# A two-layer attention trunk on one core: 22 instead of 14 opening products, and softmax sums of two heads folded together

## The chip, the cores and the metric

The kernel runs on one core of a Trainium2 chip. The metric is the time of one execution on the device in microseconds, shown for several runs. A profile of one execution gives the start and end of every instruction on TensorE (PE; its weight loads are PEld), VectorE (DVE), ScalarE (ACT), GpSimd (POOL) and SyncE (SP, which here issues all DMA transfers), and the clock that TensorE was granted.

## The reference

Input x is 2048 tokens by 1024 channels, f32. Layer A normalises x, projects it to q, k, v, one forget logit per head and a gate, normalises q and k per head, and attends causally with 16 heads of 64 channels; then output times silu(gate), output projection, residual. Layer B makes keys and values once and attends in a window of 128. The change touches layer A's attention, whose core is this:

```python
c = jnp.cumsum(log_f, axis=1)
logits = jnp.einsum('bqhd,bkhd->bhqk', qi, k) * scale
logits = logits + ci[..., :, None] - c_k[..., None, :]
logits = jnp.where(causal, logits, -jnp.inf)
p = jax.nn.softmax(logits, axis=-1)
return jnp.einsum('bhqk,bkhd->bqhd', p.astype(v.dtype), v)
```

## The kernel before, in words

One program does all: `constants`, then layer A (projections, attention, output projection), then layer B. Each f32 operand of a large product is split into a high part h that TensorE takes whole (type fp32r) and a rest lo, and a product is the sum of h·h, h·lo and lo·h: three products of 128x128 by 128x512.

**Start.** `constants` sets a tile to zero and lets TensorE multiply it by itself IDLE times (line 228), while the first transfers run. GpSimd makes masks (`select`, line 215), VectorE makes small tables from them (`fold`, `identb`, `band`, lines 239 to 254). The first projection needs weight tiles: ScalarE writes the high half (wh, line 502), VectorE the low half (wl, line 503), eight pairs for the first 128 tokens' product (line 775, psum tile b). For each block of 128 tokens ScalarE and VectorE split the transposed x (lines 395 and 396), square it (401) and sum the squares along the free axis (403, tile ro); TensorE adds up over partitions with a product by ones (line 416, psum tile pa). Pinned instructions (`keep_in_program_order`) and a scheduler that works out an order from its own costs set how these are interleaved; on the chip each engine runs its own list strictly in that order.

**Layer A's attention.** 16 heads, each with 4 chunks of 512 queries, each chunk with steps of two 128-key blocks: 20 steps a head, 320 in all (`scores`, `values`). Scores are laid out keys by queries: two products per block (lines 994 and 995, psum tile sc, three banks), exp on ScalarE (1009), high half (ScalarE, 1012), rest (GpSimd, 1013), and four products with the values three steps later (1037, psum tile pa). The row maxima that the exponent needs come from separate products and reductions a head or so ahead (949, 957, 962), and reach the operands as four small transfers (576). Diagonal blocks get the causal mask as one more product by an identity matrix: lines 999 (two blocks side by side in the last step of a chunk) and 1003. Between all that, `gate` feeds products for the gate (line 1079, psum tile pb), whose weights come in 512 KB transfers (line 1056, tile wr<-wg, two buffers).

**The sums.** A chunk's exp values are added up in an accumulator (1022), keys on partitions. At its end `sums` reduces 32x32 blocks transposed: 16 columns of partial sums per chunk, 64 per head, in the tile `part`, which holds two heads. Five steps after a head's last chunk, `recips` folds them:

```python
nc.tensor.matmul(ps, part[:, h % 2, c0:c1].rearrange("p c b -> p (c b)"), self.fold, ...)   # L922
rc = self.sb("sq", [nr, 32])
nc.vector.tensor_tensor(rc, ps, roots[:nr, 1 if c0 else 0], ALU.mult)                       # L927
nc.vector.reciprocal(rc, rc)                                                                # L928
```

The stationary operand is 64 columns of `part`, the moving one the 128x32 table `fold`; the result, 64 partitions by 32, takes a bank of sc. It is multiplied by the inverse norms of the tokens (`roots`, loaded and inverted early, lines 1112 and 1113), inverted, and stored to `rd` by SP (929). Head 15 does it in two calls, so that its last chunk alone is left at the end. The output projection reads `rd` back, for heads 0 to 3 from step 284 on.

Of the kernel before, what the change touches and what calls it, by code (L numbers as in the profile page):

```python
# [14 lines left out]
BF16 = mybir.dt.bfloat16  # L15
# [8 lines left out]
P = 128  # L24
# [4 lines left out]
H = 16  # L29
# [3 lines left out]
CH = 512  # L33
NCH = S // CH
EPS = 1e-6
NEG = -1e30
ROT = 16
# [5 lines left out]
SUM_LAG = 5  # L43
# [25 lines left out]
EARLY = 40  # L69
REST_AT = 3  # L70

IDLE = 14

VECTORS_AT = 8
ANGLES_AT = 11
# [78 lines left out]
class Trunk:  # L154
# [56 lines left out]
    def constants(self):  # L211
        nc, cp, a = self.nc, self.const, self.a

        def select(view, src, pattern, base, cm, fill):
            nc.gpsimd.affine_select(
                out=view, in_=src, pattern=pattern, compare_op=ALU.is_ge,
                fill=fill, base=base, channel_multiplier=cm,
            )

        def tile_(name, shape, dt=F32):  # L220
            return cp.tile(shape, dt, name=name, tag=name)

        idle = self.sb("sq", [P, CH], F32R)
        nc.vector.memset(f_(idle), 0.0)
        ps = self.ps("pb", [P, CH])
        for i in range(IDLE):
            self.tc.keep_in_program_order(
                nc.tensor.matmul(ps, idle[:, :P], idle, start=i == 0, stop=i == IDLE - 1)
            )

        self.ones = tile_("ones", [P, P])
        nc.gpsimd.memset(self.ones, 1.0)
        self.tri = tile_("tri", [P, P])
        select(self.tri, self.ones, [[1, P]], 0, -1, 0.0)
        self.ident = tile_("ident", [P, P])
        select(self.ident, self.tri, [[-1, P]], 0, 1, 0.0)

        self.fold = tile_("fold", [P, 32])
        nc.vector.tensor_tensor(self.fold, self.ident[:, :32], self.ident[:, 32:64], ALU.add)
        for c in (64, 96):  # L240
            nc.vector.tensor_tensor(self.fold, self.fold, self.ident[:, c : c + 32], ALU.add)
        nc.vector.tensor_single_scalar(self.fold, self.fold, 2.0, ALU.mult)
        self.identb = tile_("identb", [P, P], BF16)
        nc.vector.tensor_copy(self.identb, self.ident)

        self.mask_s = tile_("mask_s", [P, 2, P], BF16)
        nc.gpsimd.memset(self.mask_s, 0.0)
        for i in range(2):
            select(self.mask_s[:, i], self.mask_s[:, i], [[1, P]], 0, -1, NEG)

        self.band = tile_("band", [P, 2, P], BF16)
        nc.gpsimd.memset(self.band[:, 0], 0.0)
        select(self.band[:, 0, :], self.band[:, 0, :], [[-1, P]], 0, 1, NEG)
        nc.vector.tensor_tensor(self.band[:, 1], self.tri, self.ident, ALU.subtract)

        self.loads = []
        warm = tile_("warm", [P, 1])
        nc.scalar.activation(warm, self.ones[:, :1], AF.Sqrt)

        def vector(name, n, views):  # L260
            t = tile_(name, [P, n])
            for rows, src in views:
                self.loads.append((t[rows], src))
            return t

        def column(name, src, n):
            return vector(name, n, [(slice(0, P), src.rearrange("(t p) -> p t", p=P))])

        def pair_column(name, src):
            col = src.rearrange("(p o) -> p o", o=1)  # L270
            return vector(name, 1, [(slice(0, HD), col), (slice(HD, P), col)])

        def row(name, src, n):
            return vector(name, n, [(slice(0, P), src.to_broadcast([P, n]))])

        self.g_a = column("g_a", a["norm_a_g"][0], NDT)
        self.bf = row("bf", a["b_forget"], H)
        self.g_qa = pair_column("g_qa", a["qnorm_a_g"][0])
        self.g_ka = pair_column("g_ka", a["knorm_a_g"][0])
        self.g_b = column("g_b", a["norm_b_g"][0], NDT)  # L280
        self.g_kv = column("g_kv", a["kv_norm_g"], NDT)
        self.g_qb = pair_column("g_qb", a["qnorm_b_g"][0])
        self.g_kb = pair_column("g_kb", a["knorm_b_g"])
        self.sink = row("sink", a["sinks"], H)
        self.gq16 = row("gq16", a["qnorm_b_g"][:, :ROT], ROT)
# [579 lines left out]
    def attention_a(self, op):  # L865


        nc, tc, d = self.nc, self.tc, self.d
        kbt, qbt = self.sb("big", [P, 2, S], F32R), self.sb("big", [P, 2, S], F32R)
        for i in range(2):  # L870
# [6 lines left out]
            out=mask_m[:, -P:], in_=mask_m[:, -P:], pattern=[[-1, P]], compare_op=ALU.is_ge,  # L877
            fill=NEG, base=0, channel_multiplier=1,
        )
        NSB = CH // 32  # L880
        part = self.sb("part", [P, 2, NCH, NSB], bufs=1)

        roots = self.sb("ro1", [NCH * NSB, 2, 32])
        heads, state = {}, {}
        units = [(h, ch) for h in range(H) for ch in range(NCH)]
        steps = [(u, p) for u, (h, ch) in enumerate(units) for p in range(2 * ch + 2)]
# [23 lines left out]
        def sums(u):  # L910

            h, ch = units[u]
            nc.vector.tensor_reduce(
                part[:, h % 2, ch, :], state[u][0].rearrange("p (b i) -> p b i", i=32),
                AX.X, ALU.add, apply_transpose=True,
            )

        def recips(h, c0=0, c1=NCH):

            nr = (c1 - c0) * NSB  # L920
            ps = self.ps("sc", [nr, 32])
            nc.tensor.matmul(  # L922
                ps, part[:, h % 2, c0:c1].rearrange("p c b -> p (c b)"), self.fold,
                start=True, stop=True,
            )
            rc = self.sb("sq", [nr, 32])
            nc.vector.tensor_tensor(rc, ps, roots[:nr, 1 if c0 else 0], ALU.mult)  # L927
            nc.vector.reciprocal(rc, rc)  # L928
            nc.sync.dma_start(
                out=d["rd"][h, c0 * CH : c1 * CH].rearrange("(b i) -> b i", i=32), in_=rc  # L930
            )

        def max_pieces(h, ch):
# [44 lines left out]
        def scores(n, u, p):  # L978
            h, ch = units[u]
# [16 lines left out]

            if last:
                o = tiles[0].rearrange("p (b q) -> p b q", b=2)[:, :, :P]
                nc.tensor.matmul(o, self.identb, self.mask_s, start=False, stop=True)
                nc.scalar.activation(pf[:, :tw], tiles[0][:, :tw], AF.Exp, scale=HD**-0.5)  # L1000
            else:
                for n_, ps in enumerate(tiles if diag else ()):
                    mm = nc.tensor.matmul(
                        ps[:, :P], self.identb, self.mask_s[:, 0], start=False, stop=True
                    )
                    if n_:
                        tc.keep_in_program_order(mm)
                for ps, (k, q0, w, off) in zip(tiles, bl):
                    nc.scalar.activation(  # L1009
                        pf[:, off : off + w], ps[:, :w], AF.Exp, scale=HD**-0.5  # L1010
                    )
# [98 lines left out]
        for c in range(2):  # L1110
            rows = roots[: (NCH - c) * NSB, c]
            nc.sync.dma_start(out=rows, in_=d["rr"][0, c * CH :].rearrange("(b i) -> b i", i=32))
            nc.vector.reciprocal(rows, rows)
        more_pieces(1)
        per = len(pieces)

# [32 lines left out]
        for n, (u, p) in enumerate(steps):  # L1149
            h, ch = units[u]  # L1150
            if n % per_head == LOAD_AT and h + 1 < H:
                more_pieces(len(pieces) + 1)
            target = per * (n + AHEAD + 1) // per_head + 1
            ahead(target - 1)
            ends = len(pending) == V_LAG and closes(pending[0])
            if ends:
                values(pending.pop(0))
            pending.append(scores(n, u, p))
            ahead(target)
            if len(pending) > V_LAG and not ends:  # L1160
                values(pending.pop(0))
            if p == 2 * ch + 1:
                if h == H - 1 and ch in (0, NCH - 1):
                    due.append((n + SUM_LAG, (h, ch and 1, ch + 1)))
                elif ch == NCH - 1:
                    due.append((n + SUM_LAG, (h,)))
            while due and due[0][0] <= n:
                recips(*due.pop(0)[1])
            feed((total - KEPT) * (n + 1) // len(steps), pause=True)
            if n == RAW_AT:  # L1170
                raw = self.sb("big", [P, NDT // 2, D])
                for p in range(NDT // 2):
                    op.weight_load(p, raw[:, p])
            if n in PREP_AT:
                op.load(PREP_AT.index(n), ("qn", "wh", "qn", "wl"))
                op.prepare(PREP_AT.index(n), nc.gpsimd)
# [45 lines left out]
    def out_a(self, op, res, dst, ahead, fetch, norm):  # L1222
# [12 lines left out]
        for s in range(NCH * NDT):  # L1235
# [9 lines left out]
                nc.sync.dma_start(out=xr[:, p - 1], in_=res[t0 : t0 + P, :])  # L1245
            if s == NDT:

                self.gk16 = self.sb("part", [P, ROT], bufs=1)
                gk = self.a["knorm_b_g"].rearrange("(o d) -> o d", o=1)[:, :ROT]
                self.load_vectors([(self.gk16, gk.to_broadcast([P, ROT]))])  # L1250
            op.step(s)
# [391 lines left out]
```

## Time and profile before

| | |
|---|---|
| time, three runs | 2438.67, 2438.85, 2440.66 us; median 2438.85 |
| the profiled execution | 2437.35 us, of which the span is 2435.5 us |
| mean granted clock | 0.999 |
| TensorE busy | 2411.8 us, 99% of the span |
| VectorE busy | 1729.5 us, 71% |
| projections of layer A | about 9 to 593 us |
| attention of layer A | about 593 to 1450 us |
| fold products (line 922) | 17 calls from 653.2 to 1442.9 us |

A busy share is of the whole span and mixes stages with different limits; what matters for a change is which engine is waited for where it stands. A number "x14" in a row is a count of instructions, the first number of a timeline row is the start in us from the span's start, the second the duration of the merged piece, and in brackets stands the idle time before and what ended it.

### The profile page before, as it was taken

The page shows a single profiled execution, that of the slowest core. Times are in us where ns is not written, and L with a number is a line of the kernel's source. Part 1 is how long each engine was busy: PE and PEld are TensorE (multiplying, and loading weights), DVE is VectorE, ACT ScalarE, POOL GpSimd, SP SyncE. Part 2 cuts the span into 40 slices and gives each one's busy share as a digit, 9 for nine tenths or more (in the row PEclk, how much of TensorE's full clock was granted, in tenths as well). Part 3 has the DMA queues.
Part 4 walks back from the last instruction along what each step waited for, and adds up shares of the span by engine and source line. Part 5 has one row for each costly group of instructions (what it writes and reads, how often), then busy time and mean ns, then how long its engine had stood idle before and what let it go on. Part 6 is the DMA issues. An engine that isn't in the chain of part 4 may idle for free.

```text
span 2435.5 us, 36294 instructions
## 1 busy us (share of the span) xinstructions
PE 2411.8 (99%) x11966; PEld 2028.7 (83%) x11966; DVE 1729.5 (71%) x4099; ACT 1261.4 (52%) x2504; POOL 999.5 (41%) x643
## 2 busy tenths in 40 slices
PE   9999999999999999999999999999999999999999
PEld 7888899987888788888888878888888888888887
DVE  7756567735999888888888865556766523777776
ACT  5433324323878778777877761135322312555554
POOL 0000000011878777777778852200011000477775
PEclk9999999999999999999999999999999999999999
DMA  6656545677554655575466559965433425555552
GB/s 191 205 163 195 156 149 169 195 244 234 162 166 131 204 157 146 147 211 175 131 195 173 170 143 312 298 230 160 126 101 107 139 68 163 180 179 178 178 182 74
DMA packets 351516, 419.24 MB, mean 172 GB/s; under 512 B 64928, under 2 KB 248256, under 8 KB 345152
## 3 DMA queue, kind: packets, MB, share of 16 engines
q1 hardware_dynamic: 351328, 416.92, 57.4%
q8 instruction: 95, 1.56, 0.3%
q14 instruction: 93, 0.76, 0.1%
HBM read 265.29 MB, written 151.40 MB: 171 GB/s over the span
## 4 chain that ended last, share of the span: by engine, by line
PE 89%; DVE 4%; DMA 3%; ACT 2%; POOL 1%; issue 1%; SPq 0%; DVEq 0%; ACTq 0%; POOLq 0%
PE b L775 30%; PE pa L1037 10%; PE pb L1079 7%; PE b L1260 5%; PE sc L994 5%; PE sc L995 5%; PE mx L949 5%; PE pb L1473 5%; PE pb L738 3%; PE b L738 3%; PE pa L1403 2%; PE b L1324 2%; PE pa L359 1%; PE pa L1260 1%; PE pb L359 1%
## 5 line engine op out<-in xcount | busy, mean ns | idle before, releaser
L775 PE MATMUL b<-wh,big 128*128 128x512 f32 (+3 forms) x2560 | 772.2, 375 | 3.0 <-ACT wh L502 2.4
L1013 POOL TENSOR_TENSOR big<-st,big 128x1024 fp32r<-128x1024 f32 (+1 forms) x320 | 656.0, 2070 | 242.9 <-ACT big L1012 161.3
L775 PEld LDWEIGHTS b<-wh,big 128*128 128x128 f32 x2560 | 471.4, 188 | 75.2 <-ACT wh L502 4.8
L775 PE MATMUL b<-wl,big 128*128 128x512 f32 (+3 forms) x1280 | 474.1, 371 | 0.8 <-DVE wl L503 0.8
L1022 DVE TENSOR_TENSOR ac<-ac,st 128x512 f32<-128x512 f32 (+3 forms) x576 | 352.5, 612 | 51.9 <-ACT st L1009 24.3
L1009 ACT ACTIVATE st<-sc 128x512 f32<-128x512 f32 (+1 forms) x512 | 273.7, 582 | 117.6 <-PE sc L995 48.6
L1037 PE MATMUL pa<-big 128*128 128x512 f32 (+3 forms) x1280 | 320.5, 366 | 0.6 <-POOL big L1013 0.6
L1012 ACT CAST big<-st 128x1024 fp32r<-128x1024 f32 (+1 forms) x320 | 295.2, 923 | 8.5
L775 PEld LDWEIGHTS b<-wl,big 128*128 128x128 f32 x1280 | 241.7, 189 | 35.9 <-DVE wl L503 3.5
L1037 PEld LDWEIGHTS pa<-big 128*128 128x128 f32 x1280 | 229.9, 190 | 39.2 <-POOL big L1013 2.2
L962 DVE TENSOR_REDUCE mt<-mx 128x1 f32<-128x384 f32 (+1 forms) x360 | 214.2, 598 | 29.7 <-PE mx L949 27.1
L511 ACT ACTIVATE sq<-b,r 128x512 f32<-128x512 f32 (+2 forms) x128 | 77.8, 608 | 302.8 <-PE b L775 299.8
L994 PE MATMUL sc<-big 128*128 128x512 f32 (+3 forms) x640 | 233.2, 368 | 1.1 <-DVE st L558 1.1
L995 PE MATMUL sc<-big 67*128 67x512 f32 (+3 forms) x640 | 229.4, 367 | 0.0
L949 PE MATMUL mx<-big 66*128 66x512 f32 (+2 forms) x600 | 224.7, 379 | 0.2
L1079 PE MATMUL pb<-wh,wr 128*128 128x512 f32 x488 | 178.6, 398 | 3.3 <-DMA wr<-wg 3.2
L513 DVE TENSOR_REDUCE sm<-sq 128x8 f32<-128x512 f32 (+2 forms) x128 | 74.9, 585 | 139.3 <-ACT sq L511 139.1
L875 POOL MEMSET rot<- 128x512 bf16 x1 | 0.5, 525 | 418.6 <-PE pb L359 418.6
L1372 POOL TENSOR_TENSOR big<-big,tri 128x1024 fp32r<-128x1024 f32 x60 | 143.8, 2397 | 67.1 <-DVE big L1369 62.2
L957 DVE CUSTOM_DVE_ANT_0 mx<-mx,rot 128x384 f32<-128x384 f32 (+2 forms) x240 | 146.9, 617 | 20.1 <-PE mx L949 19.3
L994 PEld LDWEIGHTS sc<-big 128*128 128x128 f32 x640 | 121.9, 190 | 23.0 <-DVE st L558 1.5
L526 POOL TENSOR_TENSOR ro<-qn,rot 128x64 f32<-128x64 f32 (+1 forms) x48 | 15.7, 328 | 298.2 <-DVE qn L517 298.2
(284 smaller groups left out, 4237.8 us busy)
## 6 DMA issues: line engine op xcount, KB each, us to landing
wr<-wg SPq DMA_DIRECT2D x62, 512.0 KB
va<-st SPq DMA_DIRECT2D x32, 512.0 KB
ka<-st SPq DMA_DIRECT2D x64, 256.0 KB
ut<-big SPq DMA_DIRECT2D x16, 1024.0 KB
big<-ka SPq DMA_DIRECT2D x16, 1024.0 KB
big<-qa SPq DMA_DIRECT2D x16, 1024.0 KB
qb<-st SPq DMA_DIRECT2D x64, 256.0 KB
big<-qb SPq DMA_DIRECT2D x16, 1024.0 KB
```

The source lines that it names most:

```text
L775: nc.tensor.matmul(ps[:, :n], u[tb // 4][:, dt, us], W[k][dt], start=(dt == 0 and i == 0), stop=(dt == NDT - 1 and i == 2),)
L949: mm = nc.tensor.matmul(ps, qb[:66, i * P : (i + 1) * P], kb[:66, k0:k1], start=True, stop=True,)
L957: nc.vector.tensor_tensor_reduce(out=ps, in0=ps, in1=mask_m[:, 512 - w :], scale=1.0, scalar=NEG, op0=ALU.add, op1=ALU.max, accum_out=f_(o),)
L962: nc.vector.reduce_max(o, ps, axis=AX.X)
L994: nc.tensor.matmul(o, ka[:, ks], qa[:, qs], start=not (last and n_), stop=False)
L995: nc.tensor.matmul(o, kb[:, ks], qb[:, qs], start=False, stop=not diag)
L1009: nc.scalar.activation(pf[:, off : off + w], ps[:, :w], AF.Exp, scale=HD**-0.5)
L1012: nc.scalar.copy(ph[:, :tw], pf[:, :tw])
L1013: nc.gpsimd.tensor_tensor(pl[:, :tw], pf[:, :tw], f_(ph[:, :tw]), ALU.subtract)
L1022: nc.vector.tensor_tensor(a_, a_, pf[:, off : off + w], ALU.add)
L1037: nc.tensor.matmul(pv[:, q0 : q0 + w], v[:, k, :], src[:, off : off + w], start=(p == 0 and n_ == 0 and i == 0), stop=(last and n_ == 1 an ...
L1079: nc.tensor.matmul(ps, w[:, dt // 2 % 2, wk, dt % 2, :], us[dt][uk], start=(dt == 0 and i == 0), stop=(dt == NDT - 1 and i == 2),)
```

## The change

It sets IDLE to 22. It keeps one mask tile instead of two copies and reads it twice by a view with a step of zero. And `recips` takes n heads at once: for heads 1, 3, ... 13 it folds the head before and this one with a stationary operand of 128 columns, multiplies and inverts 128 partitions, and stores both; head 14 alone and head 15 in two calls as before. `part` has two tiles now, and `roots` holds a second copy of the inverse norms in the upper 64 partitions.

```diff
-IDLE = 14
+IDLE = 22
...
-        self.mask_s = tile_("mask_s", [P, 2, P], BF16)
+        self.mask_s = tile_("mask_s", [P, P], BF16)
         nc.gpsimd.memset(self.mask_s, 0.0)
-        for i in range(2):
-            select(self.mask_s[:, i], self.mask_s[:, i], [[1, P]], 0, -1, NEG)
+        select(self.mask_s, self.mask_s, [[1, P]], 0, -1, NEG)
...
-        part = self.sb("part", [P, 2, NCH, NSB], bufs=1)
-        roots = self.sb("ro1", [NCH * NSB, 2, 32])
+        part = [self.sb("part", [P, 2, NCH, NSB], bufs=2) for _ in range(2)]
+        roots = self.sb("ro1", [P, 2, 32])
...
-        def recips(h, c0=0, c1=NCH):
-            nr = (c1 - c0) * NSB
+        def recips(h, c0=0, c1=NCH, n=1):
+            nr = n * (c1 - c0) * NSB
...
-                ps, part[:, h % 2, c0:c1].rearrange("p c b -> p (c b)"), self.fold,
-                start=True, stop=True,
+                ps,
+                part[h // 2 % 2][:, h % 2 : h % 2 + n, c0:c1].rearrange("p n c b -> p (n c b)"),
+                self.fold, start=True, stop=True,
...
-                out=d["rd"][h, c0 * CH : c1 * CH].rearrange("(b i) -> b i", i=32), in_=rc
+                out=d["rd"][h : h + n, c0 * CH : c1 * CH].rearrange("n (b i) -> n b i", i=32),
+                in_=rc,
...
-                nc.tensor.matmul(o, self.identb, self.mask_s, start=False, stop=True)
+                m = self.mask_s.unsqueeze(1).to_broadcast([P, 2, P])
+                nc.tensor.matmul(o, self.identb, m, start=False, stop=True)
...
+        nc.sync.dma_start(out=roots[NCH * NSB :, 0], in_=d["rr"][0].rearrange("(b i) -> b i", i=32))
+        nc.vector.reciprocal(roots[NCH * NSB :, 0], roots[NCH * NSB :, 0])
...
-                elif ch == NCH - 1:
+                elif ch == NCH - 1 and h == H - 2:
                     due.append((n + SUM_LAG, (h,)))
+                elif ch == NCH - 1 and h % 2:
+                    due.append((n + SUM_LAG, (h - 1, 0, NCH, 2)))
```

The scheduler works the order out anew. Line numbers of the changed kernel are one less than before from 249 to 922, and one to three more from `scores` on. At the start, VectorE's list before:

```order
L503 SCALAR_TENSOR_TENSOR wl<-big,g_a,wh 128x512 x3
L239 TENSOR_TENSOR fold<-ident 128x32
L244 CAST identb<-ident 128x128
L241 TENSOR_TENSOR fold<-fold,ident 128x32
L254 TENSOR_TENSOR band<-tri,ident 128x128
L241 TENSOR_TENSOR fold<-fold,ident 128x32
L503 SCALAR_TENSOR_TENSOR wl<-big,g_a,wh 128x512
L242 TENSOR_SCALAR fold<-fold 128x32
L503 SCALAR_TENSOR_TENSOR wl<-big,g_a,wh 128x512 x4
L396 TENSOR_TENSOR big<-wr,big 128x8x128
```

and now:

```order
L502 SCALAR_TENSOR_TENSOR wl<-big,g_a,wh 128x512 x2
L239 TENSOR_TENSOR fold<-ident 128x32
L244 CAST identb<-ident 128x128
L241 TENSOR_TENSOR fold<-fold,ident 128x32
L253 TENSOR_TENSOR band<-tri,ident 128x128
L241 TENSOR_TENSOR fold<-fold,ident 128x32
L502 SCALAR_TENSOR_TENSOR wl<-big,g_a,wh 128x512
L242 TENSOR_SCALAR fold<-fold 128x32
L502 SCALAR_TENSOR_TENSOR wl<-big,g_a,wh 128x512 x5
L395 TENSOR_TENSOR big<-wr,big 128x8x128
```

The third low half now stands behind five of the small tables instead of before them, the fourth behind all six. On TensorE the list at the start differs only in `x22` for `x14`.

At the first fold, five steps into head 1 (the sums of head 0), TensorE's list before:

```order
L1003 MATMUL sc<-mask_s,identb 128x128
L949 MATMUL mx<-big 128x512
L922 MATMUL sc<-fold,part 64x32
L1079 MATMUL pb<-wh,wr 128x512
L1079 MATMUL pb<-wl,wr 128x512
L949 MATMUL mx<-big 128x512
```

and now:

```order
L1005 MATMUL sc<-mask_s,identb 128x128
L950 MATMUL mx<-big 128x512
L1081 MATMUL pb<-wh,wr 128x512
L1081 MATMUL pb<-wl,wr 128x512
L950 MATMUL mx<-big 128x512
```

The fold is gone and its neighbours stand as they did. Later in head 9, after the fold of head 8 that is gone too, TensorE's list before (scores of a diagonal step, then gate products):

```order
L994 MATMUL sc<-big 128x384
L995 MATMUL sc<-big 128x384
L1003 LDWEIGHTS identb
L1003 MATMUL sc<-mask_s,identb 128x128
L1003 LDWEIGHTS identb
L1003 MATMUL sc<-mask_s,identb 128x128
L949 MATMUL mx<-big 128x384
L1079 MATMUL pb<-wh,wr 128x512
L1079 MATMUL pb<-wl,wr 128x512
L1079 MATMUL pb<-wh,wr 128x512 x2
L1079 MATMUL pb<-wl,wr 128x512
L1079 MATMUL pb<-wh,wr 128x512 x2
```

and now:

```order
L995 MATMUL sc<-big 128x384
L1081 MATMUL pb<-wh,wr 128x512
L1081 MATMUL pb<-wl,wr 128x512
L1081 MATMUL pb<-wh,wr 128x512 x2
L1081 MATMUL pb<-wl,wr 128x512
L1081 MATMUL pb<-wh,wr 128x512 x2
L996 MATMUL sc<-big 128x384
L1005 LDWEIGHTS identb
L1005 MATMUL sc<-mask_s,identb 128x128
L1005 LDWEIGHTS identb
L1005 MATMUL sc<-mask_s,identb 128x128
L950 MATMUL mx<-big 128x384
```

Seven gate products came forward over one score product, two mask products and a maximum. Two or three more places shift by a few rows in this way.

More of the change, by code (lines that the diff above doesn't have):

```diff
@@ L913, in sums @@
             nc.vector.tensor_reduce(
-                part[:, h % 2, ch, :], state[u][0].rearrange("p (b i) -> p b i", i=32),
+                part[h // 2 % 2][:, h % 2, ch, :], state[u][0].rearrange("p (b i) -> p b i", i=32),
                 AX.X, ALU.add, apply_transpose=True,
             )
-        def recips(h, c0=0, c1=NCH):
-            nr = (c1 - c0) * NSB
+        def recips(h, c0=0, c1=NCH, n=1):
+            nr = n * (c1 - c0) * NSB
             ps = self.ps("sc", [nr, 32])
             nc.tensor.matmul(
-                ps, part[:, h % 2, c0:c1].rearrange("p c b -> p (c b)"), self.fold,
-                start=True, stop=True,
+                ps,
+                part[h // 2 % 2][:, h % 2 : h % 2 + n, c0:c1].rearrange("p n c b -> p (n c b)"),
+                self.fold, start=True, stop=True,
             )
@@ L1003, in scores @@
                     mm = nc.tensor.matmul(
-                        ps[:, :P], self.identb, self.mask_s[:, 0], start=False, stop=True
+                        ps[:, :P], self.identb, self.mask_s, start=False, stop=True
                     )
@@ L1246, in out_a @@
             if s == NDT:
-                self.gk16 = self.sb("part", [P, ROT], bufs=1)
+                self.gk16 = self.sb("part", [P, ROT], bufs=2)
                 gk = self.a["knorm_b_g"].rearrange("(o d) -> o d", o=1)[:, :ROT]
```

## The prediction

> **What bounds the kernel now.** I read the page's busy table and chain first, then TensorE's waits by stage, then the start in single instructions.
>
> ```profile
> span 2435.5 us, 36294 instructions
> PE 2411.8 (99%) x11966; PEld 2028.7 (83%) x11966; DVE 1729.5 (71%) x4099; ACT 1261.4 (52%) x2504; POOL 999.5 (41%) x643
> PE 89%; DVE 4%; DMA 3%; ACT 2%; POOL 1%; issue 1%; SPq 0%; DVEq 0%; ACTq 0%; POOLq 0%
> ```
>
> The chain runs through TensorE for 89% of the span. In layer A's attention, where the sums are folded, TensorE is nearly everything: of 857 us it is busy 852.5, and its waits are small.
>
> ```profile
> 593.00:1450.00 857.00, 852.52 (x4158) 704.49 (x4158) 743.20 (x1627) 672.94 (x1063) 667.39 (x330) 1.00 0.58 167
> ...
> PE pb L1079 <- DMA wr<-wg: 3.2, 3, 1.4
> PE sc L994 <- DVE st L558: 1.1, 1, 1.1
> PE pa L1037 <- POOL big L1013: 0.6, 2, 0.3
> ```
>
> So in that stage an instruction taken off TensorE shortens the run by about its own time, and one taken off VectorE (743 of 857 busy) by nothing. The start is different. In the two queries below (TensorE and VectorE in order of time; then stretches, whose first column is TensorE's busy time and whose third number from the end is the granted clock):
>
> ```profile
> 1.53 5.38 PE L228 MATMUL pb<-sq 128*128 128x512 f32 x14 [1.53 <-DVE sq L224]
> 8.66 0.49 PE L775 MATMUL b<-wh,big 128*128 128x512 f32 x1 [1.75 <-ACT wh L502]
> ...
> 20.11 0.39 PE L775 MATMUL b<-wl,big 128*128 128x512 f32 x1
> 20.93 0.38 PE L416 MATMUL pa<-ones,ro 128*128 128x1 f32 x2 [0.43 <-DVE ro L403]
> ```
> ```profile
> 8.64 2.08 DVE L503 SCALAR_TENSOR_TENSOR wl<-big,g_a,wh 128x512 fp32r<-128x512 f32 x3 [2.12 <-ACT wh L502]
> ...
> 12.03 2.73 DVE L503 SCALAR_TENSOR_TENSOR wl<-big,g_a,wh 128x512 fp32r<-128x512 f32 x4
> 14.68 1.22 DVE L396 TENSOR_TENSOR big<-wr,big 128x1024 fp32r<-128x1024 f32 x1
> ...
> 18.90 1.98 DVE L403 TENSOR_REDUCE ro<-wr 128x128 f32<-128x1024 f32 x1
> ```
> ```profile
> 7.00:9.00 2.00, 0.34 (x1) 0.19 (x1) 0.36 (x1) 1.11 (x2) 0.00 (x0) 1.00 1.06 410
> 9.00:12.40 3.40, 3.11 (x8) 2.37 (x8) 3.40 (x11) 3.40 (x7) 0.00 (x0) 0.51 1.04 419
> 12.40:20.90 8.50, 8.10 (x36) 6.25 (x35) 8.50 (x9) 6.54 (x7) 0.00 (x0) 0.99 0.18 74
> 20.90:107.00 86.10, 86.06 (x392) 71.49 (x393) 65.77 (x112) 44.11 (x58) 0.00 (x0) 1.00 0.67 194
> ```
>
> The fourteen zero products end at 6.91, TensorE stands for 1.75 us until ScalarE has made the first weight tile, and then eight products run at half clock (0.51 from 9.0 to 12.4). But VectorE has no gap from 8.64 to 20.88 (3.40 of 3.40, then 8.50 of 8.50), and TensorE stops at 20.5 to wait 0.43 us for its second block sum (L403). Only after 20.93 is TensorE full (86.06 of 86.10). The end of the start stage is therefore set by the first weights' arrival and twelve microseconds of VectorE.
>
> **Part 1: 22 zero products.** In a steady stretch a 512-column product takes 0.23 us from start to start:
>
> ```profile
> 650.94 0.39 PE L1079 MATMUL pb<-wh,wr 128*128 128x512 f32 x1
> 651.17 0.40 PE L949 MATMUL mx<-big 66*128 66x512 f32 x1
> ...
> 652.81 0.47 PE L949 MATMUL mx<-big 66*128 66x512 f32 x1
> 653.21 0.30 PE L922 MATMUL sc<-fold,part 128*64 128x32 f32 x2
> 653.44 0.50 PE L1079 MATMUL pb<-wh,wr 128*128 128x512 f32 x1
> 653.78 0.39 PE L1079 MATMUL pb<-wl,wr 128*128 128x512 f32 x1
> ```
>
> Eight more end at 6.91 + 8 x 0.23 = 8.75 if they run at that pace, or at 6.91 + 8 x 0.38 = 9.98 at the mean of the first fourteen (5.38 / 14). The first real product is then between 0.1 and 1.3 us late. Behind it stand 41 products and one pair of sums up to the wait at 20.93: 41 x 0.23 + 0.2 = 9.6 us at full clock, so TensorE reaches that wait at 18.4 to 19.6 by its own pace, a little later where a weight tile holds it, but ahead of 20.89. The wait grows, the end stays. VectorE's own work there is the same number of instructions; the order moves one low-half split (wl) behind the small constants, which takes nothing away. I take 0.0 for this part. Its ends: +0.1, if the moved split delays VectorE a little, and -1.6, the 8 half-clock products at 0.43 instead of 0.23, if TensorE were the bound after all.
>
> **Part 2: sums folded in pairs.** Before, a fold is called once for each of heads 0 to 14 and twice for head 15. Now heads 0/1 to 12/13 share one call each: 14 calls become 7, the other three stay. One call's price is read from the rows above: from the start of the maximum's product (652.81) to the start of the second gate product (653.78) pass 0.97 us; two ordinary products in that place are 0.46. The fold costs 0.51 us of TensorE, far over its 32 columns, since it goes in two passes with a weight load each (34 of them for 17 calls in the next row). A pair loads 128 columns instead of 64:
>
> ```profile
> L922 PEld LDWEIGHTS sc<-fold,part x34: 93/133/136, 653.2 to 1442.9; 128*64 128x64 f32 x30, 128*16 128x16 f32 x2, 128*48 128x48 f32 x2
> L416 PEld LDWEIGHTS pa<-ones,ro x32: 186/188/192, 18.0 to 96.3; 128*128 128x128 f32 x32
> ```
>
> 188 - 133 = 55 ns more, twice: 0.11, a pair costs 0.62. The sum is 7 x 0.62 - 14 x 0.51 = 4.34 - 7.14 = -2.8 us. Ends: -3.6 (the longer loads lie beside other products) and 0 (a pair costs as much as two folds). I take -2.8, nearest to the rows of loads.
>
> VectorE loses 7 x (173 + 334) ns and SP seven small transfers:
>
> ```profile
> L927 DVE TENSOR_TENSOR sq<-sc,ro x17: 171/173/184, 654.5 to 1445.2; 64x32 f32<-64x32 f32 x15, 16x32 f32<-16x32 f32 x1, 48x32 f32<-48x32 f32 x1
> L928 DVE RECIPROCAL sq<-sq x17: 332/334/345, 655.2 to 1445.4; 64x32 f32<-64x32 f32 x15, 16x32 f32<-16x32 f32 x1, 48x32 f32<-48x32 f32 x1
> ```
>
> Neither is waited for by TensorE, except through the gate weights below: 0. If VectorE had hidden stalls there, it could give up to the 0.6 + 1.1 us of the non-DMA waits above; I leave that in the range. The even head's reciprocals reach memory one head later; the first that are read back, those of heads 0 to 3, are loaded at step 284 of 320, ten heads after they are stored. The last three calls, which the end of the stage waits for, are unchanged.
>
> The added root load and reciprocal (upper 64 partitions) stand early in layer A's projections, where VectorE waits anyway:
>
> ```profile
> DVE sm L513 <- ACT sq L511: 4.7, 3, 2.4
> ...
> DVE ro L1113 <- DMA ro<-rr: 0.5, 1, 0.5
> ```
>
> One more reciprocal (0.34 us each there) and perhaps one more 0.5 us wait go into these 4.7 us of VectorE's idle time between 110 and 130: 0. If that cover were gone, the normalised keys of one block would be late next, and TensorE's transposes of them, which stand a block later in its order.
>
> **Part 3: the mask's single copy.** The last diagonal product reads one 128-column mask twice by a zero step, where it read 256 stored columns:
>
> ```profile
> L999 PE MATMUL sc<-mask_s,identb x64: 283/284/288, 594.8 to 1432.5; 128*128 128x256 bf16 x64
> L1003 PE MATMUL sc<-mask_s,identb x128: 219/224/233, 593.8 to 1430.6; 128*128 128x128 bf16 x128
> ```
>
> The trace has no TensorE operand with a zero step. As many columns go through: 0, the lower end; the upper end, if each column were read at half the rate, is another 256 columns, 0.12 us (half of 0.23) x 64 = 7.7 us. I take 0, nearest to a rate of 60 ns per 128 columns that these two rows give. The GpSimd select that goes is done by 2.6 us, long before use.
>
> **Part 4: order.** At most removed folds next to nothing else moves. At one place (head 9, behind the removed fold of head 8) seven gate products come forward over a score product, a mask pair and a maximum, and the load they wait for does not come earlier:
>
> ```profile
> 1092.15 0.34 PE L994 MATMUL sc<-big 128*128 128x384 f32 x1
> 1092.33 0.34 PE L995 MATMUL sc<-big 67*128 67x384 f32 x1
> ...
> 1092.61 0.42 PE L949 MATMUL mx<-big 66*128 66x384 f32 x1
> 1093.09 0.50 PE L1079 MATMUL pb<-wh,wr 128*128 128x512 f32 x1
> ```
>
> They stood at 1093.09, 0.48 us after a 384-column product where the step from 1092.15 to 1092.33 is 0.18: a wait of 0.3 us. Now they are wanted at 1092.3, so this wait may grow by up to 0.7. In head 5 a gate load goes ahead of a value load on SP, at a place without a wait. I take +0.3 for both, ends -0.3 and +0.7.
>
> **Sum:** 0.0 - 2.8 + 0 + 0.3 = -2.5 us. The profiled execution took 2437.35 us (span 2435.5), which becomes 2434.8; the median of the runs shown is 2438.85, 1.5 above it, and becomes 2436.3, 0.10% less.
>
> **Rivals.**
> *The zero products pay too.* For it: eight products at half clock. The Trainium skill (TensorE: Matmul & The Clock Gate, "What's actually happening") says the clock is gated by a free-running activity window of about 3.4 us, so work that fills the pause should hold full clock. The rows agree with it: 1.75 us of pause, then 3.4 us at 0.51. Against it as a gain: the 0.43 us wait for VectorE at 20.93. With -1.6 more: 2434.7.
> *The gate weights' stall goes.* One stall costs far more than the others:
>
> ```profile
> 801.80 0.81 PE L1037 MATMUL pa<-big 128*128 128x512 f32 x3
> 804.04 0.53 PE L1079 MATMUL pb<-wh,wr 128*128 128x512 f32 x1 [1.44 <-DMA wr<-wg]
> ...
> 804.38:807.80 3.42, 3.42 (x12) 2.94 (x11) 1.16 (x3) 0.42 (x1) 0.63 (x1) 0.50 0.63 152
> ```
>
> 1.44 us of waiting, then 12 products in 3.42 us at half clock, about 1.2 us lost. If the shift of less than 1 us by then lets the load land in time, 2.6 more go: 2433.7, faster. Against it: the load is issued behind row maxima that move with TensorE.
> *The moved products stall.* If the load at 1093 is late by another 0.7 and the pause again halves the clock (1.2): -2.5 + 1.6 = 2437.9, no change.
> *The other side: the zero step is read slowly.* At half rate +7.7 gives 2444.0, slower; it decides from (2.5 + 4.9) / 64 = 0.12 us for each of the 64 products. Nothing in the rows speaks for it.
> *The change does nothing:* the pair costs two folds, 2439.1.
>
> **How the numbers follow.** This kernel's runs lie within 2 us, so 0.2%, 4.9 us, is about what can be told from no change. My forecast has 0.60; zero products paying 0.10 (same side of the bound, unless the stall goes too: 0.02 of it faster); the stall going 0.12, faster; moved products stalling 0.07, the pair as dear as two folds 0.05, both within the bound; slow mask 0.06, slower. Faster 0.14, same 0.80, slower 0.06. The range takes in the stall's end and the pair's end with a little run scatter: 2433.2 to 2439.4.
>
> **What the profile after would show.** Start: no pause before the first real product, no half-clock stretch at 9 to 12, and the second sum's wait (L416's place) ending at 20.9 as before, grown from 0.43 to about 1 us. That wait gone, or ending earlier, proves part 1 wrong. Attention: 20 passes of the fold instead of 34, those of pairs with 188 ns loads; the mask's product still 284 ns; TensorE's busy time lower by 2 to 3 us from 593 to the stage's end. DMA waits of more than 4 us in sum would break the forecast.

## The result and the profile after

The changed kernel takes 2433.25 us (median of 18 runs, 2431.52 to 2438.86), the kernel before 2437.68 us beside it (18 runs, 2433.24 to 2440.98). The ratio is 0.9984, 95% interval 0.9977 to 0.9990: 3.9 us less, between 2.4 and 5.6. The forecast was 2.5 less; the interval's lower end just reaches it, and the reason is below.

The page after, the same rows as before:

```profile
span 2431.0 us, 36257 instructions
PE 2406.9 (99%) x11960; PEld 2027.7 (83%) x11960; DVE 1730.6 (71%) x4086; ACT 1260.0 (52%) x2504; POOL 997.5 (41%) x642
PE 90%; DVE 4%; DMA 3%; ACT 2%; issue 1%; POOL 1%; SPq 0%; ACTq 0%; DVEq 0%; POOLq 0%
```

TensorE lost 4.9 us of busy time, and the span 4.5. The start in order of time (TensorE, then VectorE), and as stretches:

```profile
1.53 7.50 PE L228 MATMUL pb<-sq 128*128 128x512 f32 x22 [1.53 <-DVE sq L224]
8.86 0.39 PE L774 MATMUL b<-wh,big 128*128 128x512 f32 x1
...
17.77 0.35 PE L415 MATMUL pa<-ones,ro 128*128 128x1 f32 x2 [0.34 <-DVE ro L402]
...
20.70 0.38 PE L415 MATMUL pa<-ones,ro 128*128 128x1 f32 x2 [0.38 <-DVE ro L402]
```
```profile
8.45 1.41 DVE L502 SCALAR_TENSOR_TENSOR wl<-big,g_a,wh 128x512 fp32r<-128x512 f32 x2 [1.88 <-ACT wh L501]
...
18.68 1.97 DVE L402 TENSOR_REDUCE ro<-wr 128x128 f32<-128x1024 f32 x1
```
```profile
7.00:9.00 2.00, 2.00 (x10) 1.50 (x8) 0.56 (x1) 1.31 (x3) 0.00 (x0) 1.00 1.05 407
9.00:12.40 3.40, 3.11 (x13) 1.90 (x12) 3.40 (x11) 3.40 (x7) 0.00 (x0) 1.00 1.04 420
12.40:20.70 8.30, 7.59 (x33) 5.36 (x31) 8.30 (x9) 6.33 (x7) 0.00 (x0) 1.00 0.18 72
```

The pause before the first real product is gone, and there is no half-clock stretch (1.00 where 0.51 stood); whether the one follows from the other is taken up with the first experiment. It bought nothing: VectorE is as full as it was, its chain starts 0.2 us earlier with the first weights, and the second block sum's product starts those 0.2 us earlier (20.70 instead of 20.93) after a wait. From VectorE's first low half to that product pass 12.3 us in both (8.64 to 20.93 before, 8.45 to 20.70 now).

A fold of a pair of heads, TensorE's products and then its weight loads; and the loads of a single head's fold before:

```profile
811.93 0.48 PE L950 MATMUL mx<-big 66*128 66x512 f32 x1
812.25 0.30 PE L921 MATMUL sc<-fold,part 128*128 128x32 f32 x2
812.39 0.48 PE L1081 MATMUL pb<-wh,wr 128*128 128x512 f32 x1
812.71 0.39 PE L1081 MATMUL pb<-wl,wr 128*128 128x512 f32 x1
```
```profile
811.91 0.19 PEld L950 LDWEIGHTS mx<-big 66*128 66x128 f32 x1
812.02 0.42 PEld L921 LDWEIGHTS sc<-fold,part 128*128 128x128 f32 x2
```
```profile
813.59 0.19 PEld L949 LDWEIGHTS mx<-big 66*128 66x128 f32 x1
814.02 0.19 PEld L922 LDWEIGHTS sc<-fold,part 128*64 128x64 f32 x2 [0.24 <-issue]
```

From the maximum's product to the second gate product pass 0.773 us (811.93 to 812.71), where 0.974 were before. The pair is not dearer than a single fold but cheaper: 0.31 instead of 0.51 beyond two ordinary products. The loads show where. The pair's first load begins 0.11 us after the load before it, while the product before still runs; the narrow one, of 64 columns, began 0.43 us after, with 0.24 us of idle time, together with its own product.

TensorE's waits in the attention, the gate weights first:

```profile
PE pb L1081 <- DMA wr<-wg: 3.3, 4, 1.3
PE sc L995 <- DVE st L557: 1.1, 1, 1.1
```

They did not grow in this run. The products that moved in head 9 start at 1089.21 without a wait, since their load went out at 1084.00 instead of 1087.90 (TensorE's rows, then SP's):

```profile
1089.04 0.34 PE L995 MATMUL sc<-big 128*128 128x384 f32 x1
1089.21 0.40 PE L1081 MATMUL pb<-wh,wr 128*128 128x512 f32 x1
```
```profile
1084.00 0.54 SPq L1058 DMA_DIRECT2D wr<-wg  x1
```

### The profile page after: what moved, and what is told of

The parts are those of the page before. It is cut to its first block, busy times and chain, and to the rows that moved or that the text cites. A ratio compares the mean times of both kernels' runs of the same rounds, so it can differ in the third digit from the quotient of the medians.

```text
span 2431.0 us, 36257 instructions
## 1 busy us (share of the span) xinstructions
PE 2406.9 (99%) x11960; PEld 2027.7 (83%) x11960; DVE 1730.6 (71%) x4086; ACT 1260.0 (52%) x2504; POOL 997.5 (41%) x642
## 4 chain that ended last, share of the span: by engine, by line
PE 90%; DVE 4%; DMA 3%; ACT 2%; issue 1%; POOL 1%; SPq 0%; ACTq 0%; DVEq 0%; POOLq 0%
PE b L774 30%; PE pa L1039 10%; PE pb L1081 7%; PE b L1266 5%; PE pb L1479 5%; PE sc L995 5%; PE sc L996 5%; PE mx L950 5%; PE pb L737 3%; PE b L737 3%; PE pa L1409 2%; PE b L1330 2%; PE pb L358 1%; DVE wl L502 1%; PE pa L358 1%
## 5 line engine op out<-in xcount | busy, mean ns | idle before, releaser
L996 PEld LDWEIGHTS sc<-big 67*128 67x128 f32 x640 | 122.1, 191 | 19.2
```

Of the source, the lines that this page charges most:

```text
L996: nc.tensor.matmul(o, kb[:, ks], qb[:, qs], start=False, stop=not diag)
```

## Experiments

**The opening products alone.**

```diff
-IDLE = 14
+IDLE = 22
```

> The kernel before with 22 opening products instead of 14 and nothing else; TensorE's order is otherwise the same. Theory (the start is set by the first weights and by VectorE's chain): no difference, within 0.5 us; no half-clock stretch between 9 and 12.5 us, but the second block sum's product still starts at 20.7 to 21.0 us. Rival (the cold products were paid for): 1.6 us faster, and that product starts near 19.4.

Ratio 1.0003 (0.9994 to 1.0012), 2437.28 beside 2436.76 us. There is no half-clock stretch, and the second sum waits, as in the changed kernel:

```profile
1.53 7.41 PE L228 MATMUL pb<-sq 128*128 128x512 f32 x22 [1.53 <-DVE sq L224]
...
20.70 0.38 PE L416 MATMUL pa<-ones,ro 128*128 128x1 f32 x2 [0.41 <-DVE ro L403]
```

A gain of 1.6 us (ratio 0.9993) lies just outside the interval. The rival falls, and a second figure speaks against it: from VectorE's first low half to the second sum's product pass 12.26 to 12.30 us in every profile with 14, 22 or 40 opening products, with and without the half-clock stretch (the bf16 kernel below, which makes one more small table on VectorE, has 12.35).

That the 22 products keep the clock up is not shown. The five profiles with 22 or 40 have no half-clock stretch at the start, but of the seven profiles of kernels with 14 opening products only the first, of the kernel before, has the stretch. The next experiment but one stands longer before its first real product, 1.93 instead of 1.75 us, and then goes at full pace (0.23 us from start to start; granted clock 1.00 from 9.0 to 12.4):

```profile
8.45 0.50 PE L778 MATMUL b<-wh,big 128*128 128x512 f32 x1 [1.93 <-ACT wh L505]
...
10.04 0.39 PE L778 MATMUL b<-wl,big 128*128 128x512 f32 x1
10.27 0.63 PE L778 MATMUL b<-wh,big 128*128 128x512 f32 x2
```

**The rest alone.** The changed kernel with `IDLE = 14`.

> The changed kernel with 14 opening products; TensorE's order is otherwise that of the changed kernel. If the whole gain is the folds' (7 x 0.31 - 14 x 0.51 = -5.0 us by the profile after) it is as fast as the changed kernel: ratio to before 0.998, -4 to -5 us. If the opening products carry part of the gain, it keeps only the rest: -2.8 to -3.4 us.

Ratio 0.9989 (0.9980 to 0.9998), 2433.30 us. The gain is in this part, but its size, 2.7 us with an interval of 0.5 to 4.9, doesn't separate the two expectations.

**One head to a fold, but 128 columns loaded.**

```diff
+        part = [self.sb("part", [P, 2, NCH, NSB], bufs=2) for _ in range(2)]
+        for t in part:
+            nc.gpsimd.memset(t[:, 1], 0.0)
...
+            cols = WIDTH(h) if nr == NCH * NSB else nr
+            ps = self.ps("sc", [cols, 32])
+            flat = part[h % 2].rearrange("p k c b -> p (k c b)")
...
+                ps, flat[:, c0 * NSB : c0 * NSB + cols], self.fold, start=True, stop=True
```

`WIDTH(h)` is 128.

> The kernel before (14 opening products, each head folded by itself), but the fold of heads 0 to 14 loads 128 columns, the upper 64 zero (the single mask tile pays for the space). Theory (a stationary operand of the full 128 columns is loaded beside the product before it, a narrower one is not): each of 15 folds costs 0.31 instead of 0.51 us of TensorE, start of the product before to start of the second one after 0.77 instead of 0.97; 3.0 us faster than before although nothing is saved in calls. Rival (a fold's price follows from its count, more columns only cost more): 15 x 0.11 = 1.7 us slower, 0.97 or more between those starts.

The price is as the theory has it. Its TensorE rows:

```profile
653.01 0.47 PE L956 MATMUL mx<-big 66*128 66x512 f32 x1
653.33 0.30 PE L929 MATMUL sc<-fold,part 128*128 128x32 f32 x2
653.47 0.48 PE L1087 MATMUL pb<-wh,wr 128*128 128x512 f32 x1
653.78 0.39 PE L1087 MATMUL pb<-wl,wr 128*128 128x512 f32 x1
```

0.77 us with as many calls as before: the width does it, not the count. The time did not follow: ratio 0.9998 (0.9989 to 1.0007), 0.5 us less, and the 3.0 expected lie just outside (the medians, 2435.15 and 2436.76 us, lie 1.6 apart). By the profile its waits for the gate weights were 4.6 us instead of 3.2, so a part was given back there. The attention is still 2.5 us shorter in it (848.8 instead of 851.3, table below), but from the last fold to the end, where no product was changed, it took 995.3 us instead of 992.7, and 990.4 to 993.5 in the other profiles. Why is open; the profiled execution is the slowest but one of eleven.

**At what width.** Two kernels, each with its own list of loaded columns by head.

```diff
+WIDTHS = (64, 72, 80, 88, 96, 104, 112, 116, 120, 122, 124, 125, 126, 127, 128)
...
+    return WIDTHS[h]
```

> As the previous one, with another number of loaded columns in each head, in order of heads 0 to 14: 64, 72, 80, 88, 96, 104, 112, 116, 120, 122, 124, 125, 126, 127, 128. Theory (only the full width is loaded ahead): the fold's price grows with the columns from 0.51 at 64 to about 0.6 at 127 and falls to 0.31 at 128. Rival A: it falls step by step, or at another width (96, say). Rival B: no fall, the price after came from the place of the folds and not from their width.

The theory was wrong in its width. From the maximum's product to the second gate product pass 0.975 us at 64 columns, 0.745 at 88, 0.752 at 104, 0.761 at 120 and 0.773 at 128; already at 72 and 80, with other neighbours, it is cheap (0.476 and 0.805, where 64 columns in the same places took 0.722 and 0.974 before). So the second list asks for the step. The single executions took 2436.21 us and, with the second list, 2434.98.

> As the sweep before, with loaded columns 64, 65, 66, 67, 68, 70, 72, 64, 65, 66, 68, 72, 80, 64, 65 in heads 0 to 14. The sweep showed 0.51 at 64 and 0.28 to 0.35 from 72 on. Theory (64 columns and fewer are a form of their own): 64 dear at heads 0, 7 and 13, and every other width cheap from 65 on, about 0.27. Rival (a step at a multiple of 4 or 8, or the place in the program): 65 to 67 as dear as 64, or head 7 or 13 cheap.

```profile
1024.11 0.47 PE L959 MATMUL mx<-big 66*128 66x512 f32 x1
1024.52 0.30 PE L932 MATMUL sc<-fold,part 128*64 128x32 f32 x2
1024.75 0.50 PE L1090 MATMUL pb<-wh,wr 128*128 128x512 f32 x1
1025.09 0.39 PE L1090 MATMUL pb<-wl,wr 128*128 128x512 f32 x1
```
```profile
1078.09 0.47 PE L959 MATMUL mx<-big 66*128 66x512 f32 x1
1078.41 0.25 PE L932 MATMUL sc<-fold,part 128*65 128x32 f32 x2
1078.49 0.48 PE L1090 MATMUL pb<-wh,wr 128*128 128x512 f32 x1
1078.81 0.39 PE L1090 MATMUL pb<-wl,wr 128*128 128x512 f32 x1
```

Heads with 64 columns: 0.975, 0.974 and 0.974 us. With 65: 0.718 and 0.719; 67, 68, 70 and 72: 0.715 to 0.726. One column more makes the fold 0.256 us cheaper among gate products; where its neighbours are others, 65 to 68 columns are 0.17 to 0.26 cheaper than 64 were before in the same places.

**Is it the type?** The kernel before with the single mask tile and the sums rounded to bf16, columns 64, 65, 64, 128, 65, ... by head.

```diff
...
+            nc.vector.tensor_copy(thin[:, :nr], part[:, h % 2, c0:c1].rearrange("p c b -> p (c b)"))
+            nc.tensor.matmul(ps, thin[:, :cols], self.foldb, start=True, stop=True)
```

> The kernel before with the single mask tile, each head's sums rounded to bf16 in a tile of 128 columns (so the result keeps fewer digits) and folded with a bf16 table: one pass instead of two. Loaded columns for heads 0 to 14: 64, 65, 64, 128, 65, 64, 72, 128, 64, 65, 64, 128, 65, 64, 96. Theory (64 columns and fewer are dear whatever the type): the heads with 64 cost 0.1 us or more over those with 65, from the start of the product before to that of the second after. Rival (it belongs to plain f32 and its two passes): no difference beyond 0.02 us between 64 and 65.

```profile
651.50 0.47 PE L953 MATMUL mx<-big 66*128 66x512 f32 x1
651.90 0.20 PE L928 MATMUL sc<-foldb,thin 128*64 128x32 bf16 x1
652.03 0.50 PE L1084 MATMUL pb<-wh,wr 128*128 128x512 f32 x1
652.37 0.40 PE L1084 MATMUL pb<-wl,wr 128*128 128x512 f32 x1
```
```profile
864.75 0.47 PE L953 MATMUL mx<-big 66*128 66x512 f32 x1
865.06 0.18 PE L928 MATMUL sc<-foldb,thin 128*65 128x32 bf16 x1
865.09 0.47 PE L1084 MATMUL pb<-wh,wr 128*128 128x512 f32 x1
865.40 0.39 PE L1084 MATMUL pb<-wl,wr 128*128 128x512 f32 x1
```

0.87 us at 64, 0.65 at 65 (0.67 at 128). The step is there in bf16 and one pass too. The one execution took 2443.15 us beside 2439.91. TensorE waits in it for one rounded copy (1.5 us), for the maxima (3.1) and for the gate weights (7.6 instead of 3.2); how much of that the added copies on VectorE bring is not shown.

**The mask alone.**

```diff
-        self.mask_s = tile_("mask_s", [P, 2, P], BF16)
+        self.mask_s = tile_("mask_s", [P, P], BF16)
...
-                nc.tensor.matmul(o, self.identb, self.mask_s, start=False, stop=True)
+                m = self.mask_s.unsqueeze(1).to_broadcast([P, 2, P])
+                nc.tensor.matmul(o, self.identb, m, start=False, stop=True)
```

> The kernel before with the single mask tile alone; TensorE's order is unchanged. Theory: no difference (within 0.5 us), the two-block mask product 284 ns as before. Rival (the zero step is read slowly): up to 7.7 us slower, that product 340 ns or more. Its distance from before also shows how far two kernels of equal work lie apart.

Ratio 1.0001 (0.9992 to 1.0010), and the product takes what it took:

```profile
L999 PE MATMUL sc<-mask_s,identb x64: 283/284/287, 594.7 to 1433.4; 128*128 128x256 bf16 x64
```

**How much room the start has.** The changed kernel with 2 and with 40 opening products, one execution each (2435.87 and 2440.47 us, beside 2439.91 of before).

> The changed kernel with 2 opening products. They end near 2.5 us; the real ones start near 8.2 at half clock. Theory (start set by the weights' arrival and VectorE): one half-clock stretch of up to 3.4 us costs 9 products about 0.2 us each, no more than with 14, and the second block sum's product starts at 20.3 to 20.9 us as in all the others; if two stretches pass before the clock is released, up to 0.9 us later. Rival (the opening products matter): that product starts at 22 us or later.

> The changed kernel with 40 opening products: they end near 1.5 + 10 x 0.43 + 30 x 0.23 = 12.7 us, so the first real product is about 4 us late. Behind it stand 41 products and a pair of sums, 9.6 us: TensorE becomes what the second block sum's product waits for, which starts near 22.3 us instead of 20.3 to 20.9. If it starts there all the same, TensorE has more slack than I reckoned.

With 2, eleven products and part of a twelfth run at half pace, 0.43 us from start to start, until 13.5 us (the clock record of this run begins only there, so the pace has to stand for it). TensorE comes to the second sum 0.1 us after VectorE has it, without a wait:

```profile
8.17 0.80 PE L774 MATMUL b<-wh,big 128*128 128x512 f32 x1 [5.42 <-ACT wh L501]
...
20.34 0.39 PE L774 MATMUL b<-wl,big 128*128 128x512 f32 x1
20.56 0.29 PE L415 MATMUL pa<-ones,ro 128*128 128x1 f32 x2
```

From VectorE's first low half to this product pass 12.41 us, 0.1 more than in the other kernels: so even twelve products at half pace cost next to nothing up to there, and there the room ends. With 40 the first real product starts at 13.17, and the second sum still at 20.50: the scheduler had put 29 products ahead of it instead of 41. The price comes behind: the attention's first score starts at 599.6 us, in the other kernels at 590 to 592. Since the order is another one, this is no clean measure of the room.

**Folds of full width only.** Heads 14 and 15 in two products of 128 columns instead of three of 64, 16 and 48; and the changed kernel again on the same chip.

```diff
-            ps = self.ps("sc", [nr, 32])
+            ps = self.ps("sc", [P, 32])
...
+            nc.vector.tensor_tensor(rc[r0:r1], ps[r0:r1], roots[r0:r1, 0], ALU.mult)
...
+                    due.append((n + SUM_LAG + 3, (h // 2, 0, NCH * NSB + NSB)))
```

> The changed kernel, with heads 14 and 15 folded in two products of the full 128 columns instead of three of 64, 16 and 48: nine wide folds in all, and one load and one reciprocal of inverse norms less. If what makes a fold dear is the narrow stationary operand (0.31 us wide, 0.51 narrow), three narrow ones (about 1.3 us) become two wide ones (0.6): 0.6 to 0.9 us less than the changed kernel, 5 to 6 us less than before if no wait takes it back. Rival (a shorter TensorE only waits longer for the gate weights): no difference to the changed kernel within 0.5 us, and the waits for them in the attention grow above 4 us.

> The changed kernel itself, on the same chip as the others of this call: 3 to 5 us less than before (ratio 0.998 to 0.9988).

2433.62 us (ratio 0.9980, 0.9971 to 0.9989) against 2434.83 (0.9985, 0.9976 to 0.9994), beside 2437.61 of before. Its ratio is the lowest here and it lies 1.2 us below the changed kernel, but the intervals overlap, so that step isn't shown, and the rival stays possible. Both profiles have more waiting than the first one of the changed kernel, 5.4 us with all folds wide and in the repeat 6.1 instead of 3.3, with a half-clock stretch at 718 (the repeat's rows):

```profile
PE pb L1081 <- DMA wr<-wg: 6.1, 7, 1.8
...
714.00:722.00 8.00, 6.25 (x23) 4.89 (x22) 4.13 (x9) 4.94 (x7) 5.59 (x4) 0.79 0.44 64
```

Set against each other, the profiles give the gain of the attention, from the first score's start to the last fold's (the last column takes off the waits for gate weights, and 1.5 us where a half-clock stretch fell in the stage: the same eleven products take 3.59 us from 804.38 before and 2.06 from 804.22 in the changed kernel; the prediction's estimate was 1.2):

| kernel | stage, us | waits for gate weights | half clock | left |
|---|---|---|---|---|
| before | 851.3 | 3.2 | once | 846.6 |
| 22 products alone | 850.3 | 4.2 | no | 846.1 |
| mask alone | 852.3 | 4.4 | no | 847.9 |
| changed | 845.8 | 3.3 | no | 842.5 |
| changed, again | 851.1 | 6.1 | once | 843.5 |
| changed, 14 products | 847.4 | 4.5 | no | 842.9 |
| one head, 128 columns | 848.8 | 4.6 | no | 844.2 |
| all folds wide | 849.9 | 5.4 | once | 843.0 |

Single folds of 64 columns leave 846.9 in the mean (three rows), pairs 843.0 (three): 3.9 us, as the timing says, though prices alone make it 14 x 0.51 - 7 x 0.31 = 5.0. About 1 us is unaccounted for; rows of equal work differ by 1.0 to 1.8 us, so that it is hardly outside their scatter. One head with 128 columns lies 2.7 below the single folds, near the 3.0 that its prices make.

## Why the prediction was right, and where its size was off

- *The time*: 2433.25 us lies 0.05 inside the stated range, at an end that was kept for the gate weights' stall going. The stall didn't go, so that the time lies inside is luck. Of the 3.1 us below the forecast of 2436.3, 1.2 are the base: the kernel before took 2437.68 in 18 runs, where the prediction started from 2438.85. Its runs lie within 7.7 us of each other, not within 2.
- *The start is set by the weights and VectorE*: right, term 0.0. Shown by the 22 products alone (between 1.5 us less and 2.9 more), by the wait that stays at 20.70 and by the 12.3 us from VectorE's first low half. The growth of that wait to about 1 us did not come: it split into two, 0.34 us at the first sum and 0.38 at the second. The half-clock stretch was read as what the pause brings, from one profile; the others don't bear that out.
- *A fold costs 0.51 us*: right, for 64 columns.
- *"A pair costs 0.62"*: this term failed. I added the longer loads; the pair costs 0.31. The width makes it cheap, as one head with 128 columns and the step from 64 to 65 show. In the traces a stationary operand of 65 or 128 columns is loaded beside the product before it, one of 64 together with its own product; that this late load is the cause of the price, and not another effect of the width, is not shown. Both ends that I kept (a pair as dear as one fold, or as two) lay on the wrong side. The term was -2.8 and by prices is -5.0.
- *The moved products wait up to 0.7 longer (+0.3)*: wrong, no wait. Their load went out earlier as well: 3.9 us, against the 3.1 by which TensorE was ahead (1089.04 instead of 1092.15 for the score product before them).
- *The mask*: right, 0.
- *The gate weights' stall goes* (rival): it didn't, it is 1.30 us at 803.88; but no half-clock stretch followed it this time. By what was measured in the stage I can't say what decides that.

The two misses, -2.2 and -0.3, are larger than the difference of 1.4 us between forecast and measurement; the rest is the microsecond that stays open. The terms of the start and of the mask, and that TensorE is the bound in the attention, held.

The Trainium skill (TensorE: Matmul & The Clock Gate, "LDWEIGHTS (loading the stationary operand)") gives a load's time in ns as its columns divided by 1.2; by that, 64 columns more are an estimate of 53 ns. The trace agrees in the difference, 133 ns at 64 and 190 at 128, but not in the proportion: some 80 ns stand on top of the formula in both, and here the measurement decides. The price on the path goes the other way, it falls from 0.51 to 0.31 us.

## What to carry to other kernels

Price an instruction by the starts of its neighbours, at the shape it will have: the same operation with twice the columns was cheaper, and no row of the old shape could show it. Products at half clock are worth avoiding only where TensorE is what the next instruction waits for; look first for the wait that ends the stage. A product whose stationary operand has 64 columns, among ordinary ones of 128, is worth padding to more, if TensorE is the bound. The last fold, of 48, shows the same: 0.862 us from the product before to the second one after, and 0.680 with 128 columns and the same neighbours in the kernel with all folds wide.

## What was not expected of the hardware

- The step from 64 to 65 loaded columns: 0.256 us less for a two-pass f32 product among ordinary ones (0.974 to 0.718), 0.22 us for a bf16 one in one pass (0.87 to 0.65). Three things are later at 64: the product itself (0.41 us after the one before, at 65 it is 0.32), the second pass or the next product, and the product after it (0.34, then 0.32). The first product of 128 columns behind a fold of 64 is loaded late too, together with its start. Why the step is at 64 was not tried further.
- The same program, profiled twice, waited 3.3 and 6.1 us for the same loads, and its attention took 845.8 and 851.1 us. A single profile of this kernel says little about 3 us.
- The length of a pause doesn't decide by itself whether half clock follows: it followed 1.44 us of waiting at 804.04 in the kernel before, and did not follow 1.30 at 803.88 in the changed kernel or 1.93 at the start of one head with 128 columns. In each trace the granted clock changes on a grid of 3.41 us: in the kernel before at 5.66, 9.08, 12.49, 804.38 and 807.80, and from 9.08 to 804.38 are 233 such steps of 3.413. What within a step decides is open.
